# Differential attention on Trainium2: the scores of both maps on half the array each, queries and keys loaded whole, values stored by head

## The chip, the cores and the metric

The kernel runs on one core of a Trainium2 chip. The metric is device time in microseconds (us) for one execution; three runs of the kernel before are given, and one further execution was recorded by the hardware profiler. Engines are named as in the profile: PE is TensorE (matmuls), PEld its weight loads, DVE is VectorE, ACT is ScalarE, POOL is GpSimd, and SP (SyncE) is the queue from which nearly all DMA transfers are issued.

## The reference

The program is one layer of a decoder with 1024 positions and a model width of 1024. A normalized input is projected to three branches (a gated MLP over chunks, a pooling mixer and a causal differential attention), the branches are weighted by gates and projected, and a gated feed-forward layer follows. The change concerns the attention. Each of 4 heads has two maps (c = 0, 1) with 64 columns of query and key each, and one value of 128 columns:

```python
def block(args):
    qi, i = args                                   # one block of 128 queries
    ...
    s = jnp.einsum('bqhcd,bkhcd->bhcqk', qi, k).astype(jnp.float32) * scale
    s = s + bias.transpose(2, 0, 1)[None, :, None]
    s = jnp.where((rel >= 0)[None, None, None], s, -1e30)
    p = jax.nn.softmax(s, axis=-1)
    a = p[:, :, 0] - lam * p[:, :, 1]
    return jnp.einsum('bhqk,bkhd->bqhd', a.astype(v.dtype), v)
```

## The kernel before

A product of two fp32 matrices is made of fp32r matmuls: each operand is split into a high part (hi, the value rounded to fp32r) and a low part (lo, the rest), and three of the four products are added up (PASSES: hi x hi, hi x lo, lo x hi). All the large products use Strassen's scheme and run on L191.

Ahead of the attention, `store_qk` writes queries and keys of a head to DRAM (qk_d), hi and lo apart, 128 rows each: rows 0 to 63 belong to the first map, rows 64 to 127 to the second. `values` writes the value of all heads, position by position, to v_d. `rel_bias` makes the position bias with three small matmuls of 33 rows (L390); the bias tile T of a head is read back from DRAM (fsc).

The attention stage works on 32 tiles: 4 heads times 8 blocks of 128 queries, in an order given by hand (`tiles`). A tile whose block is number i has W = 128 (i + 1) key columns, in chunks of at most 512. For a tile and a map, `scores` takes a PSUM bank per chunk, and two matmuls of 128 rows: the stationary operand qs holds the map's query hi in rows 0 to 63 and lo in rows 64 to 127; the moving operand kh holds the key's hi twice, kl its lo twice. So each matmul adds two of the four products. VectorE adds the bias and finds the row's minimum in one instruction (a custom reduction, L762), and frees the bank; ScalarE does the exponential (L768).

`combine` (VectorE) subtracts the second map from the first, `transpose` turns the result on TensorE (tile at, L1103) and ScalarE copies it (ah), and `attend` multiplies it with the values (tile ms, L1112; an fp32 product, which the trace shows as two matmuls each). Between them one step of `merge_ab`, the filler, is issued per tile: six matmuls of the merge of the other two branches into a bank mm (L191), whose result VectorE multiplies into the gates ga or gb (L1179). `sub_norm` normalizes a head's output and transposes it (L1140), into a bank mm too. In each pass of the loop the steps are called in this order: scores of map 0, transpose, filler, scores of map 1, combine of the tile before, transpose. A scheduler then settles the order on each engine, as the operands become ready by its own reckoning; engines execute that order as it stands. The eight PSUM banks of the stage are 3 for scores, 2 at, 1 ms, 2 mm. The first tile's first scores are issued earlier, inside the last Strassen product of the stage before, into banks called m.

`load_head` is called one head ahead. It loads into a pool of 34 buffers of 512 KB (`a4`), each SP transfer in the order in which it stands. After the tiles `merge_c` merges the attention branch (L1204), and the product with w_out begins.

Of the kernel before, what the change touches and what calls it, by code (L numbers as in the profile page):

```python
# [11 lines left out]
F32 = mybir.dt.float32  # L12
I32 = mybir.dt.int32
F32R = mybir.dt.float32r
AF = mybir.ActivationFunctionType
# [3 lines left out]
P = 128  # L19
# [3 lines left out]
NH = 512  # L23
DFF = 2816
FT = DFF // P
NHEAD = 4
# [21 lines left out]
def trunk_kernel(  # L48
# [34 lines left out]
    def a4(shape=None, dt=F32, n="a"):  # L83
        return ap_.tile(shape or [P, S], dt, tag="a", name=nm(n))
# [7 lines left out]
    def tiny(n, tag, bufs=4):  # L92
        return sm.tile([P, n], F32, tag=tag, name=nm(tag), bufs=bufs)
# [398 lines left out]


    qk_d = dram.tile([8, 2, P, S], F32, name="qk_d")
    v_d = dram.tile([8, P, NH], F32, name="v_d")
    y_d = dram.tile([4, P, S], F32, name="y_d")
    g_d = dram.tile([24, P, S], F32, name="g_d")
    x1_d = dram.tile([KT, P, S], F32, name="x1_d")
# [3 lines left out]
    def values():  # L502

        (a11, a12), (a21, a22) = w_V
        TT, sub = nc.vector.tensor_tensor, ALU.subtract

        def operand(raw):
            hi, lo = w4(dt=F32R, n="wh"), w4(dt=F32R, n="wl")
            split(hi, lo, raw)
            return hi, lo  # L510

        def prod(banks, w, tn, first, more):
            for t in range(4):
                for j in range(4):
                    x, y = [o[:, t * P:(t + 1) * P] for o in h.T[j][tn]], wsl(w, j, 256)
                    dst = banks[t // 2][:, t % 2 * 256:t % 2 * 256 + 256]
                    if first and j == 0 and t % 2 == 0:

                        opens = nc.tensor.matmul(dst, lhsT=x[0], rhs=y[0], start=True, stop=False,
                                                 skip_group_check=True)  # L520
                    elif first and j == 0:
                        with tc.issue_after(opens.ins):
                            nc.tensor.matmul(dst, lhsT=x[0], rhs=y[0], start=False, stop=False, skip_group_check=True)
                    if first and j == 0:
                        for a, b in PASSES[1:]:
                            nc.tensor.matmul(dst, lhsT=x[a], rhs=y[b], start=False, stop=False, skip_group_check=True)
                    else:
                        mm3(dst, x, y, False, j == 3, True)

        def copies(dst, banks):  # L530
            for b in range(2):
                nc.scalar.copy(dst[b], banks[b])
            return dst

        def store(o, banks, c, r, i):

            for b in range(2):
                TT(out=o[b], in0=banks[b], in1=c[b], op=ALU.add)
                for t in range(2):
                    sl = o[b][:, t * 256:(t + 1) * 256]  # L540
                    nc.scalar.mul(sl, sl, R8[:, 4 * i + 2 * b + t:4 * i + 2 * b + t + 1])
                tt = 4 * i + 2 * b
                nc.sync.dma_start(out=v_d[tt:tt + 2, :, r * 256:(r + 1) * 256].rearrange("t p c -> p t c"),
                                  in_=o[b].rearrange("p (t c) -> p t c", t=2))

        def wide(n):
            t = w4([P, 2, NH], n=n)
            return [t[:, 0, :], t[:, 1, :]]

        A11, A12 = operand(a11), operand(a12)  # L550
        b1, b2 = ([pb1() for _ in range(2)] for _ in range(2))
        prod(b1, A11, "B11", True, True)
        c1 = copies([c2("v") for _ in range(2)], b1)
        yield
        s1, s2 = w4(n="s1"), w4(n="s2")
        TT(out=s1, in0=a21, in1=a22, op=ALU.add)
        TT(out=s2, in0=s1, in1=a11, op=sub)
        prod(b2, A12, "B21", True, False)
        store(c1, b2, c1, 0, 0)
        S1 = operand(s1)  # L560
        yield
        b3 = [pb1() for _ in range(2)]
        prod(b3, S1, "T1", True, True)
        S2 = operand(s2)
        TT(out=a21, in0=a11, in1=a21, op=sub)
        TT(out=a12, in0=a12, in1=s2, op=sub)
        yield
        prod(b1, S2, "T2", False, True)
        k2 = copies(wide("c2"), b1)
        S3 = operand(a21)  # L570
        yield
        prod(b1, S3, "T3", False, True)
        k3 = copies(wide("c3"), b1)
        store([c2("v") for _ in range(2)], b3, k3, 1, 1)
        A22 = operand(a22)
        yield
        b4 = [pb1() for _ in range(2)]
        prod(b4, A22, "T4", True, False)
        store(k3, b4, k3, 1, 0)
        S4 = operand(a12)  # L580
        yield
        prod(b3, S4, "B22", False, True)
        store(k2, b3, k2, 0, 1)
        yield
# [121 lines left out]

    def load_head(hd):

        H = heads[hd] = dict(qkl=[])
        for c in range(2):  # L710
            q, kh, kl = (a4(dt=F32R, n=n) for n in ("qs", "kh", "kl"))
            r = slice(64 * c, 64 * c + 64)
            for dst, src in ((q[0:64], qk_d[hd, 0, r]), (q[64:128], qk_d[hd, 1, r]),
                             (kh[0:64], qk_d[4 + hd, 0, r]), (kh[64:128], qk_d[4 + hd, 0, r]),
                             (kl[0:64], qk_d[4 + hd, 1, r]), (kl[64:128], qk_d[4 + hd, 1, r])):
                nc.sync.dma_start(out=dst.bitcast(F32), in_=src)
            H["qkl"].append((q, kh, kl))
            if c == 0:
                H["T"] = a4(n="T")
                base = fsc[hd]  # L720
                skew = bass.AP(tensor=base.tensor, offset=base.offset + P - 1, ap=[[NREL - 1, P], [1, S]])
                nc.sync.dma_start(out=H["T"], in_=skew)
            yield
        H["V"] = a4([P, 8, P], n="V")
        nc.sync.dma_start(out=H["V"], in_=v_d[:, :, hd * P:(hd + 1) * P].rearrange("t p c -> p t c"))
        yield
        H["s0"], H["ss"] = tiny(8, "s0", 2), tiny(8, "so", 2)
        H["O"] = a4([P, 8, P], n="O")
# [7 lines left out]
    st, AH = {}, {}  # L736
    score_bank = [pm1]

    def scores(t, c):

        if t >= len(tiles):
            return
        hd, i = tiles[t]
        H = heads[hd]
        W = (i + 1) * P
        if c == 0:
            if W <= NH:
                b = a4([P, 2, NH], n="sc")
                st[t] = dict(pr=[b[:, 0, :], b[:, 1, :]], s=[])
            else:  # L750
                st[t] = dict(pr=[a4(n="sc"), a4(n="sc")], s=[])
        q, kh, kl = H["qkl"][c]
        sc_ = st[t]["pr"][c]
        mx = tiny(2, "mx")
        chunks = [(0, min(NH, W))] + ([(NH, W - NH)] if W > NH else [])
        for n_, (c0, n) in enumerate(chunks):
            ps = score_bank[0]()
            qs = q[:, i * P:(i + 1) * P]
            nc.tensor.matmul(ps[:, :n], lhsT=qs, rhs=kh[:, c0:c0 + n], start=True, stop=False)  # L759
            nc.tensor.matmul(ps[:, :n], lhsT=qs, rhs=kl[:, c0:c0 + n], start=False, stop=True)  # L760
            o = (7 - i) * P + c0
            nc.vector.tensor_tensor_reduce(  # L762
                out=sc_[:, c0:c0 + n], in0=ps[:, :n], in1=H["T"][:, o:o + n], scale=1.0,
                scalar=mx[:, 0:1] if n_ else 3.0e38,
                op0=ALU.add, op1=ALU.min, accum_out=mx[:, n_:n_ + 1])
        nm_ = mx[:, n_:n_ + 1]
        sum_ = H["s0"][:, i:i + 1] if c == 0 else tiny(1, "s1")
        nc.scalar.activation(out=sc_[:, :W], in_=sc_[:, :W], func=AF.Exp, bias=nm_, scale=-1.0, accum_out=sum_)  # L768
        st[t]["s"].append(sum_)

    for n_ in range(12):
        Fs = strassen_pair(w_gate[n_], h, pb1)
# [299 lines left out]
    def pt2(tag, bufs):  # L1072
        def f():
            return p2.tile([P, NH], F32, tag=tag, name=nm(tag), bufs=bufs)
        return f

    score_bank[0], pat, pms, pmm = pt2("sc", 3), pt2("at", 2), pt2("ms", 1), pt2("mm", 2)

    def combine(t):

# [115 lines left out]
    def merge_c(banks):  # L1196
        for n_, (j, m) in enumerate((j, m) for j in (1, 0) for m in range(KT)):
            for k in range(3):
                pre_c(m + k)
            ps = banks[n_ % len(banks)]()  # L1200
            for ki in range(NHEAD):
                mm3(ps, wsl(wcs[m], ki), ycv[ki][j], ki == 0, ki == NHEAD - 1)
            gc = gcs[m][:, half(j)]
            nc.vector.tensor_tensor(out=gc, in0=ps, in1=gc, op=ALU.mult)  # L1204
            accumulate(mg[m][:, half(j)], gc)
            yield

    wo = strassen_full(lambda k: mg[k], w_out, 4, xT, lambda d, j: x1[d][:, half(j)], done1)
    LL = 4
    mc = merge_c([pmm, pmm, *score_bank * 3, pat, pat])  # L1210
    lates = []
    for t in range(len(tiles) + 3):
        hd, i = tiles[min(t, 31)]
# [323 lines left out]
```

## Time and profile before

| | us |
|---|---|
| median of 3 runs | 1388.32 |
| lowest, highest | 1386.16, 1389.51 |
| profiled execution, device time | 1389.13 |
| its span in the trace | 1387.4 |
| PE busy | 1344.9 (97%) |
| DVE busy | 964.5 (70%) |
| ACT busy | 652.4 (47%) |
| POOL busy | 495.9 (36%) |

The profiled execution's device time contains its span and 1.7 us around it. Busy time of PE is the union of its matmuls, the ends of which are modelled: the length shown for one matmul (0.39 us for 512 columns) is more than the distance to the next one behind it, so a stretch in which PE is busy throughout can still hold short stalls. The score matmuls of the attention run from 436.7 to 585.5 us of the span.

### The profile page before, as it was taken

The page shows a single profiled execution, that of the slowest core. Times are in us where ns is not written, and L with a number is a line of the kernel's source. Part 1 is how long each engine was busy: PE and PEld are TensorE (multiplying, and loading weights), DVE is VectorE, ACT ScalarE, POOL GpSimd, SP SyncE. Part 2 cuts the span into 40 slices and gives each one's busy share as a digit, 9 for nine tenths or more (in the row PEclk, how much of TensorE's full clock was granted, in tenths as well). Part 3 has the DMA queues.
Part 4 walks back from the last instruction along what each step waited for, and adds up shares of the span by engine and source line. Part 5 has one row for each costly group of instructions (what it writes and reads, how often), then busy time and mean ns, then how long its engine had stood idle before and what let it go on. Part 6 is the DMA issues. An engine that isn't in the chain of part 4 may idle for free.

```text
span 1387.4 us, 17666 instructions
## 1 busy us (share of the span) xinstructions
PE 1344.9 (97%) x6454; PEld 1120.5 (81%) x6454; DVE 964.5 (70%) x1487; ACT 652.4 (47%) x1109; POOL 495.9 (36%) x327
## 2 busy tenths in 40 slices
PE   9999999999999989999999999999999999999997
PEld 7997778888887778877777888888888887878786
DVE  7985774445444879958769576666777669985853
ACT  8633343344433666723667343433343435455461
POOL 0022334455553000022221665666656640102014
PEclk9999999999999999999999999999999999999998
DMA  7023363333239898588795222212222248845853
GB/s 261 10 78 109 108 222 134 121 121 104 101 115 272 252 242 209 151 233 193 201 221 131 83 77 91 79 74 91 91 77 91 75 151 305 274 126 150 226 128 122
DMA packets 78831, 204.65 MB, mean 148 GB/s; under 512 B 8270, under 2 KB 17614, under 8 KB 78744
## 3 DMA queue, kind: packets, MB, share of 16 engines
q1 hardware_dynamic: 67224, 180.44, 39.4%
q0 software_dynamic: 11520, 23.07, 9.7%
q8 instruction: 51, 0.84, 0.2%
q14 instruction: 36, 0.29, 0.1%
HBM read 143.70 MB, written 47.46 MB: 138 GB/s over the span
## 4 chain that ended last, share of the span: by engine, by line
PE 67%; DVE 13%; DMA 10%; issue 6%; ACT 3%; POOL 1%; SPq 1%; DVEq 0%; POOLq 0%; ACTq 0%
PE b L191 59%; PE mm L191 2%; DMA fr<-in_w_down 2%; DMA pr<-in_w_proj 1%; DVE ft L97 1%; PE ms L1112 1%; DVE fw L97 1%; DMA qs<-qk_d 1%; POOL ga L104 1%; DMA fr<-in_w_out 1%; DVE sc L762 1%; DMA x<-in_xT 1%; DMA yr<-y_d 1%; PE sc L759 1%; ACT fw L96 1%
## 5 line engine op out<-in xcount | busy, mean ns | idle before, releaser
L191 PE MATMUL b<-ft,fw 128*128 128x512 f32 (+1 forms) x1308 | 293.0, 384 | 9.8 <-ACT x L912 3.4
L191 PEld LDWEIGHTS b<-ft,fw 128*128 128x128 f32 x1308 | 239.9, 189 | 60.3 <-DVE fw L97 4.0
L354 POOL TENSOR_TENSOR F<-F,RB 128x1024 f32<-128x1024 f32 x68 | 185.5, 2730 | 111.3 <-DVE F L262 110.2
L262 DVE TENSOR_TENSOR F<-b,c 128x512 f32<-128x512 f32 x152 | 100.9, 683 | 130.5 <-ACT c L281 58.3
L191 PE MATMUL b<-hb,Ah 128*128 128x512 f32 x608 | 190.2, 392 | 0.0
L191 PE MATMUL b<-T,Sh 128*128 128x512 f32 x504 | 155.8, 390 | 1.9 <-ACT c L272 1.9
L234 POOL TENSOR_TENSOR s<-r 128x512 f32<-128x512 f32 x36 | 54.4, 1512 | 224.3 <-DMA r<-in_w_up 84.2
L191 PEld LDWEIGHTS b<-hb,Ah 128*128 128x128 f32 x608 | 114.5, 189 | 24.0 <-issue 0.5
L191 PE MATMUL b<-hb,Al 128*128 128x512 f32 x304 | 119.5, 393 | 2.5 <-DVE Al L97 2.5
L97 DVE TENSOR_TENSOR Al<-r,Ah 128x1024 fp32r<-128x1024 f32 x38 | 56.1, 1476 | 94.0 <-issue 77.9
L97 DVE TENSOR_TENSOR Sl<-s,Sh 128x1024 fp32r<-128x1024 f32 x76 | 107.0, 1408 | 13.9 <-ACT Sh L96 8.5
L96 ACT CAST Sh<-s 128x1024 fp32r<-128x1024 f32 x76 | 80.0, 1052 | 75.6 <-PE b L191 43.2
L191 PEld LDWEIGHTS b<-T,Sh 128*128 128x128 f32 x504 | 94.6, 188 | 21.8 <-ACT c L272 2.4
L191 PE MATMUL b<-T,Sl 128*128 128x512 f32 x252 | 98.1, 389 | 0.0
L191 PE MATMUL b<-hb,Sh 128*128 128x512 f32 x304 | 94.1, 391 | 2.9 <-DVE F L262 2.9
L96 ACT CAST Ah<-r 128x1024 fp32r<-128x1024 f32 x38 | 39.9, 1049 | 110.9 <-PE b L191 104.0
L96 ACT CAST fw<-fr 128x512 fp32r<-128x512 f32 x90 | 54.8, 622 | 62.4 <-DVE fw L97 25.0
L191 PE MATMUL b<-Th,Sh 128*128 128x512 f32 x204 | 79.1, 391 | 0.8 <-ACT c L267 0.8
L191 PE MATMUL b<-Tl,Sh 128*128 128x512 f32 x204 | 79.5, 390 | 0.0
L191 PE MATMUL b<-Th,Sl 128*128 128x512 f32 x204 | 79.4, 389 | 0.0
L191 PEld LDWEIGHTS b<-hb,Sh 128*128 128x128 f32 x304 | 56.8, 188 | 16.6 <-DVE F L262 4.2
L191 PEld LDWEIGHTS b<-hb,Al 128*128 128x128 f32 x304 | 57.4, 189 | 15.3 <-DVE Al L97 2.9
(284 smaller groups left out, 2838.9 us busy)
## 6 DMA issues: line engine op xcount, KB each, us to landing
fr<-in_w_down SPq DMA_DIRECT2D x47, 512.0 KB, 3.8
r<-in_w_up SPq DMA_DIRECT2D x42, 512.0 KB, 3.5
r<-in_w_gate SPq DMA_DIRECT2D x24, 512.0 KB, 3.6
g_d<-F SPq DMA_DIRECT2D x24, 512.0 KB, 2.8
act_d<-cv SPq DMA_DIRECT2D x22, 512.0 KB, 2.8
act<-act_d SPq DMA_DIRECT2D x22, 512.0 KB, 7.8
fr<-in_w_out SPq DMA_DIRECT2D x18, 512.0 KB, 6.1
ssb<-sq POOLq DMA_DIRECT2D x24, 256.0 KB, 4.1
```

What stands on the lines that cost most here:

```text
L96: nc.scalar.copy(hi, src)
L97: (eng or nc.vector).tensor_tensor(out=lo, in0=src, in1=hi.bitcast(F32), op=ALU.subtract)
L104: nc.gpsimd.dma_start(out=dst, in_=src, accum_op=ALU.add)
L191: last_mm[0] = nc.tensor.matmul(ps, lhsT=w[a], rhs=x[b], start=first and i == 0, stop=last and i == 2, skip_group_check=more)
L234: eng.tensor_tensor(out=s1[:, :NH], in0=a21, in1=a22, op=ALU.add)
L262: nc.vector.tensor_tensor(out=o, in0=ps, in1=c, op=ALU.add)
L354: (eng or nc.gpsimd).tensor_tensor(out=F, in0=F, in1=RB, op=ALU.mult)
L759: nc.tensor.matmul(ps[:, :n], lhsT=qs, rhs=kh[:, c0:c0 + n], start=True, stop=False)
L762: nc.vector.tensor_tensor_reduce(out=sc_[:, c0:c0 + n], in0=ps[:, :n], in1=H["T"][:, o:o + n], scale=1.0, scalar=mx[:, 0:1] if n_ else 3.0e38,
L1112: nc.tensor.matmul(po[:, :P], lhsT=AH[t][:, kb, :], rhs=H["V"][:, kb, :], start=kb == 0, stop=kb == i)
```

## The change

Queries and keys are loaded as they lie in DRAM: one tile q with hi of both maps (rows 0 to 63 and 64 to 127), one with lo, and the same for k. `scores` is called by chunk (n_) instead of by map: it takes two banks, and issues for each of the three passes one matmul per map, of 64 rows each, map 0 on rows 0 to 63 and map 1 on rows 64 to 127. The product lo x lo is no longer computed. A chunk of both maps then takes six matmuls of 64 rows where there were four of 128. The exponential follows when the last chunk of a tile is reduced. Score banks go from 3 to 4, mm from 2 to 1. The values lie in DRAM by head, so that a head's tile V is one contiguous row of 4 KB for each partition; storing them takes two transfers where there was one.

```diff
@@ -492,7 +492,7 @@
 
 
     qk_d = dram.tile([8, 2, P, S], F32, name="qk_d")
-    v_d = dram.tile([8, P, NH], F32, name="v_d")
+    v_d = dram.tile([NHEAD, P, 8, P], F32, name="v_d")
     y_d = dram.tile([4, P, S], F32, name="y_d")
     g_d = dram.tile([24, P, S], F32, name="g_d")
     x1_d = dram.tile([KT, P, S], F32, name="x1_d")
@@ -540,8 +540,9 @@
                     sl = o[b][:, t * 256:(t + 1) * 256]
                     nc.scalar.mul(sl, sl, R8[:, 4 * i + 2 * b + t:4 * i + 2 * b + t + 1])
                 tt = 4 * i + 2 * b
-                nc.sync.dma_start(out=v_d[tt:tt + 2, :, r * 256:(r + 1) * 256].rearrange("t p c -> p t c"),
-                                  in_=o[b].rearrange("p (t c) -> p t c", t=2))
+                for k in range(2):
+                    nc.sync.dma_start(out=v_d[2 * r + k, :, tt:tt + 2, :],
+                                      in_=o[b].rearrange("p (t k c) -> p k t c", t=2, k=2)[:, k])
 
         def wide(n):
             t = w4([P, 2, NH], n=n)
@@ -706,15 +707,13 @@
 
     def load_head(hd):
 
-        H = heads[hd] = dict(qkl=[])
+        H = heads[hd] = dict(q=[], k=[])
         for c in range(2):
-            q, kh, kl = (a4(dt=F32R, n=n) for n in ("qs", "kh", "kl"))
-            r = slice(64 * c, 64 * c + 64)
-            for dst, src in ((q[0:64], qk_d[hd, 0, r]), (q[64:128], qk_d[hd, 1, r]),
-                             (kh[0:64], qk_d[4 + hd, 0, r]), (kh[64:128], qk_d[4 + hd, 0, r]),
-                             (kl[0:64], qk_d[4 + hd, 1, r]), (kl[64:128], qk_d[4 + hd, 1, r])):
-                nc.sync.dma_start(out=dst.bitcast(F32), in_=src)
-            H["qkl"].append((q, kh, kl))
+            q, k = a4(dt=F32R, n="q"), a4(dt=F32R, n="k")
+            nc.sync.dma_start(out=q.bitcast(F32), in_=qk_d[hd, c])
+            nc.sync.dma_start(out=k.bitcast(F32), in_=qk_d[4 + hd, c])
+            H["q"].append(q)
+            H["k"].append(k)
             if c == 0:
                 H["T"] = a4(n="T")
                 base = fsc[hd]
@@ -722,7 +721,7 @@
                 nc.sync.dma_start(out=H["T"], in_=skew)
             yield
         H["V"] = a4([P, 8, P], n="V")
-        nc.sync.dma_start(out=H["V"], in_=v_d[:, :, hd * P:(hd + 1) * P].rearrange("t p c -> p t c"))
+        nc.sync.dma_start(out=H["V"], in_=v_d[hd])
         yield
         H["s0"], H["ss"] = tiny(8, "s0", 2), tiny(8, "so", 2)
         H["O"] = a4([P, 8, P], n="O")
@@ -736,37 +735,43 @@
     st, AH = {}, {}
     score_bank = [pm1]
 
-    def scores(t, c):
+    def scores(t, n_):
+
 
         if t >= len(tiles):
             return
         hd, i = tiles[t]
         H = heads[hd]
         W = (i + 1) * P
-        if c == 0:
+        c0 = n_ * NH
+        n = min(NH, W - c0)
+        if n <= 0:
+            return
+        if n_ == 0:
+            st[t] = dict(s=[], mx=[tiny(2, "mx", 6) for _ in range(2)])
             if W <= NH:
                 b = a4([P, 2, NH], n="sc")
-                st[t] = dict(pr=[b[:, 0, :], b[:, 1, :]], s=[])
+                st[t]["pr"] = [b[:, 0, :], b[:, 1, :]]
             else:
-                st[t] = dict(pr=[a4(n="sc"), a4(n="sc")], s=[])
-        q, kh, kl = H["qkl"][c]
-        sc_ = st[t]["pr"][c]
-        mx = tiny(2, "mx")
-        chunks = [(0, min(NH, W))] + ([(NH, W - NH)] if W > NH else [])
-        for n_, (c0, n) in enumerate(chunks):
-            ps = score_bank[0]()
-            qs = q[:, i * P:(i + 1) * P]
-            nc.tensor.matmul(ps[:, :n], lhsT=qs, rhs=kh[:, c0:c0 + n], start=True, stop=False)
-            nc.tensor.matmul(ps[:, :n], lhsT=qs, rhs=kl[:, c0:c0 + n], start=False, stop=True)
-            o = (7 - i) * P + c0
+                st[t]["pr"] = [a4(n="sc"), a4(n="sc")]
+        ps = [score_bank[0]() for _ in range(2)]
+        for k, (a, b) in enumerate(PASSES):
+            for c in range(2):
+                r = slice(64 * c, 64 * c + 64)
+                nc.tensor.matmul(ps[c][:, :n], lhsT=H["q"][a][r, i * P:(i + 1) * P], rhs=H["k"][b][r, c0:c0 + n],
+                                 start=k == 0, stop=k == 2)
+        o = (7 - i) * P + c0
+        for c in range(2):
+            sc_, mx = st[t]["pr"][c], st[t]["mx"][c]
             nc.vector.tensor_tensor_reduce(
-                out=sc_[:, c0:c0 + n], in0=ps[:, :n], in1=H["T"][:, o:o + n], scale=1.0,
+                out=sc_[:, c0:c0 + n], in0=ps[c][:, :n], in1=H["T"][:, o:o + n], scale=1.0,
                 scalar=mx[:, 0:1] if n_ else 3.0e38,
                 op0=ALU.add, op1=ALU.min, accum_out=mx[:, n_:n_ + 1])
-        nm_ = mx[:, n_:n_ + 1]
-        sum_ = H["s0"][:, i:i + 1] if c == 0 else tiny(1, "s1")
-        nc.scalar.activation(out=sc_[:, :W], in_=sc_[:, :W], func=AF.Exp, bias=nm_, scale=-1.0, accum_out=sum_)
-        st[t]["s"].append(sum_)
+            if c0 + n == W:
+                sum_ = H["s0"][:, i:i + 1] if c == 0 else tiny(1, "s1")
+                nc.scalar.activation(out=sc_[:, :W], in_=sc_[:, :W], func=AF.Exp, bias=mx[:, n_:n_ + 1], scale=-1.0,
+                                     accum_out=sum_)
+                st[t]["s"].append(sum_)
 
     for n_ in range(12):
         Fs = strassen_pair(w_gate[n_], h, pb1)
@@ -1074,7 +1079,7 @@
             return p2.tile([P, NH], F32, tag=tag, name=nm(tag), bufs=bufs)
         return f
 
-    score_bank[0], pat, pms, pmm = pt2("sc", 3), pt2("at", 2), pt2("ms", 1), pt2("mm", 2)
+    score_bank[0], pat, pms, pmm = pt2("sc", 4), pt2("at", 2), pt2("ms", 1), pt2("mm", 1)
 
     def combine(t):
 
@@ -1207,7 +1212,7 @@
 
     wo = strassen_full(lambda k: mg[k], w_out, 4, xT, lambda d, j: x1[d][:, half(j)], done1)
     LL = 4
-    mc = merge_c([pmm, pmm, *score_bank * 3, pat, pat])
+    mc = merge_c([pmm, *score_bank * 4, pat, pat])
     lates = []
     for t in range(len(tiles) + 3):
         hd, i = tiles[min(t, 31)]
```

The order of instructions after scheduling shows what the diff alone doesn't. The first place is TensorE in the stage of the second head, at a tile of 768 columns. Before, a pair of matmuls (L759 with kh, L760 with kl) serves one map and one bank; here the second map's two chunks (512 and 256 columns), between a filler's last matmul and the value products:

```order
L191 MATMUL mm_4161<-yv_3644,ph_4014 128x512
L759 MATMUL sc_4170<-kh_3845,qs_3844 128x512
L760 MATMUL sc_4170<-kl_3846,qs_3844 128x512
L759 MATMUL sc_4174<-kh_3845,qs_3844 128x256
L760 MATMUL sc_4174<-kl_3846,qs_3844 128x256
L1112 MATMUL ms_4154<-V_3550,ah_4098 128x128 x3
```

After the change, the same tile's second chunk and the first of the next tile. The moving tile k_3776 is the key's hi and k_3854 its lo, q_3775 and q_3853 the query's; the bank tells the map: sc_4191 and sc_4243 are the first map's (rows 0 to 63), sc_4192 and sc_4244 the second's (rows 64 to 127):

```order
L191 MATMUL mm_4127<-yv_3632,ph_4033 128x512
L761 MATMUL sc_4191<-k_3776,q_3775 128x256
L761 MATMUL sc_4191<-k_3854,q_3775 128x256
L761 MATMUL sc_4191<-k_3776,q_3853 128x256
L1117 MATMUL ms_4122<-V_3548,ah_4064 128x128 x4
L761 MATMUL sc_4192<-k_3776,q_3775 128x256
L761 MATMUL sc_4192<-k_3854,q_3775 128x256
L761 MATMUL sc_4192<-k_3776,q_3853 128x256
L761 MATMUL sc_4243<-k_3776,q_3775 128x512
L761 MATMUL sc_4243<-k_3854,q_3775 128x512
L761 MATMUL sc_4243<-k_3776,q_3853 128x512
L761 MATMUL sc_4244<-k_3776,q_3775 128x512
```

The three passes of a map stand together, and full-array matmuls stand between the two maps of the first chunk, though the code issues the maps in turn. At a few places, as at the first tiles, the maps do alternate.

The second place is TensorE at the sub-norm of a head (transposes of O into a bank mm). Before, the transposes follow a pair of scores, and the filler behind them has a bank of its own:

```order
L759 MATMUL sc_4334<-kh_3845,qs_3844 128x256
L760 MATMUL sc_4334<-kl_3846,qs_3844 128x256
L1140 MATMUL mm_4288<-ident,O_3554 128x128 x4
L191 MATMUL mm_4324<-yv_3638,ph_4014 128x512
L191 MATMUL mm_4324<-yv_3639,ph_4014 128x512
```

After the change, with one bank mm, the transposes stand right behind a filler's matmuls:

```order
L191 MATMUL mm_4351<-yv_3638,ph_4033 128x512
L191 MATMUL mm_4351<-yv_3644,ph_4033 128x512
L191 MATMUL mm_4351<-yv_3645,ph_4033 128x512
L191 MATMUL mm_4351<-yv_3644,ph_4033 128x512
L1145 MATMUL mm_4374<-ident,O_3552 128x128 x4
L761 MATMUL sc_4480<-k_3776,q_3775 128x384
```

The transposes into mm_4374 can begin only when VectorE has read mm_4351.

## Rows read from the trace of the kernel before

**Rows 1.** Busy us (instructions) by stretch; then PE clock, DMA share, GB/s.

```profile
444.00:462.00 18.00, 15.67 (x57) 11.21 (x58) 15.50 (x32) 9.48 (x14) 4.79 (x2) 0.91 0.72 279
...
480.00:500.00 20.00, 14.55 (x72) 11.60 (x71) 14.24 (x43) 10.81 (x35) 0.86 (x1) 0.91 1.05 288
500.00:590.00 90.00, 89.24 (x580) 78.52 (x578) 82.69 (x278) 64.55 (x197) 4.30 (x5) 1.00 0.75 187
```

**Rows 2.** Timeline of PE from 527 us: start, length, instruction, count.

```profile
527.12 1.06 PE L1112 MATMUL ms<-V,ah 128*128 128x128 f32 x8
527.93 0.42 PE L759 MATMUL sc<-kh,qs 128*128 128x384 f32 x1
528.19 0.34 PE L760 MATMUL sc<-kl,qs 128*128 128x384 f32 x1
528.37 1.09 PE L191 MATMUL mm<-yv,ph 128*128 128x512 f32 x4
...
529.75 0.28 PE L759 MATMUL sc<-kh,qs 128*128 128x256 f32 x1
529.87 0.27 PE L760 MATMUL sc<-kl,qs 128*128 128x256 f32 x1
```

**Rows 3.** Groups of PE instructions from 500 to 590 us: busy, mean ns, idle before.

```profile
L191 PE MATMUL mm<-yv,ph 128*128 128x512 f32 x126 | 33.5, 400 | 0.0
L1112 PE MATMUL ms<-V,ah 128*128 128x128 f32 x204 | 28.5, 277 | 0.2 <-ACT sq L1117 0.2
L1103 PE MATMUL at<-ident,sc 128*128 128x128 f32 x108 | 16.5, 274 | 0.0
L759 PE MATMUL sc<-kh,qs 128*128 128x512 f32 x27 | 11.7, 434 | 0.3 <-DVE mx L762 0.2
...
L759 PE MATMUL sc<-kh,qs 128*128 128x384 f32 x10 | 3.7, 365 | 0.0
...
L759 PE MATMUL sc<-kh,qs 128*128 128x128 f32 x12 | 3.3, 272 | 0.0
```

**Rows 4.** Timeline of PE from 480 to 500 us, in brackets idle time before.

```profile
484.75 0.47 PE L760 MATMUL sc<-kl,qs 128*128 128x512 f32 x1 [1.59 <-DMA kl<-qk_d]
...
493.37 2.07 PE L191 MATMUL mm<-yv,ph 128*128 128x512 f32 x4 [3.32 <-ACT ph L96]
```

**Rows 5.** Chain that ended last, two pieces: start, us, what.

```profile
106.93 23.78 PE b L191 x110
...
480.30 12.38 DMA pr<-in_w_proj
```

**Rows 6.** Bias matmuls L390: timeline of PEld and PE; last, min, median, max ns.

```profile
130.10 0.19 PEld L191 LDWEIGHTS b<-hb,Al 128*128 128x128 f32 x1
...
130.32 0.39 PE L191 MATMUL b<-hb,Al 128*128 128x512 f32 x1
130.64 1.02 PE L390 MATMUL m<-oh,rb 33*4 33x512 f32 x2
131.59 0.73 PE L191 MATMUL b<-hb,Sh 128*128 128x512 f32 x2
...
140.15 0.39 PE L191 MATMUL b<-Th,A 128*128 128x512 f32 x1
140.47 0.38 PE L390 MATMUL m<-oh,rb 33*4 33x127 f32 x2
...
L390 PE MATMUL m<-oh,rb x6: 268/589/589, 130.6 to 140.6; 33*4 33x512 f32 x4, 33*4 33x127 f32 x2
```

**Rows 7.** Group of the filler's multiply on DVE, 436 to 592 us.

```profile
L1179 DVE TENSOR_TENSOR ga<-mm,ga 128x512 f32<-128x512 f32 x16 | 11.0, 686 | 3.2 <-PE mm L191 2.2 <-DMA ga<-g_d 1.0
```

**Rows 8.** DMA from 421 to 515 us: packets and bytes; issues of one kind.

```profile
DMA packets 9985, 24.56 MB, mean 261 GB/s; under 512 B 1056, under 2 KB 4128, under 8 KB 9980
...
kh<-qk_d SPq DMA_DIRECT2D x12, 256.0 KB, 10.1
```

**Rows 9.** Issues of value stores on SP: min, median, max ns; first, last start.

```profile
L543 SPq DMA_DIRECT2D v_d<-v x4: 360/374/390, 71.8 to 93.2; - x4
```

## The prediction

> **What bounds the kernel now.** I read the stretches first [rows 1]: between 500 and 590 us, where most score tiles are worked on, the reader is to see TensorE busy for 89.24 of 90 us, VectorE for 82.69, and the DMA engines with room (0.75). Busy can hide stalls, because the ends of matmuls are modelled, so I rebuilt those 90 us from spacings. Four matmuls of 512 columns take 1.09 us, a single one 0.39, so they follow each other by 0.23; one of 384 columns is followed after 0.18, one of 256 after 0.12; eight of 128 columns take 1.06 with a last one of 0.28, which is 0.11 each [rows 2]. Times the counts [rows 3], where the second matmul of each score pair (L760) has the counts of the first and 256 columns the count of 384: 126 x 0.23 for mm, (204 + 108) x 0.11 for ms and at, another 24 x 0.11 for the transposes of L1140, and 54, 20, 20 and 24 score matmuls at 0.23, 0.18, 0.12 and 0.11. That is 29.0 + 37.0 + 21.1 = 87 us of 90. TensorE is full there: what is added to it lengthens the kernel. VectorE has 7 us to spare.
>
> From 480 to 500 us it is otherwise: TensorE is busy for 14.55 of 20 us, and DMA is saturated at 1.05 [rows 1]. A score pair waits 1.59 us for kl, a merge matmul 3.32 us for weights [rows 4], whose load is on the chain that ended last for 12.38 us [rows 5]. From 444 to 462 us VectorE is nearly full (15.50 of 18), TensorE is not (15.67). In both stretches the mean granted clock is 0.91 [rows 1]: the lower level, 1.2 of 2.4 GHz, for part of the time.
>
> Ahead of attention and from the first w_out products on, the change leaves the order on TensorE, VectorE, ScalarE and GpSimd as it is; only SyncE's value stores differ there.
>
> **The score matmuls themselves.** Before there are 192: 12 chunks a head, two maps, two matmuls each, which is 96, 32, 32 and 32 of 512, 384, 256 and 128 columns. At the spacings above they take 22.1 + 5.8 + 3.8 + 3.5 = 35.2 us. Afterwards there are 288, each on 64 rows. The spacing goes with the columns in these rows, so without overlap they take half as much again: +17.6.
>
> How much overlaps is decided by the order: for most tiles the scheduler does not leave the two maps alternating. It issues the three passes of one map, which share 64 rows and one bank and so must follow each other, then the three of the other. Only where a matmul on the other half comes next can two run at once. In the 45 unbroken runs of score matmuls I counted 77 such neighbours: 37 of 512 columns, 19 of 384, 9 of 256, 12 of 128. No row here shows matmuls on different halves, so what one neighbour saves lies between nothing and its whole streaming time. For 512 columns that is 37 x 0.23 = 8.5 us. Each matmul needs its weight load, and the runs of 128 columns show that loads come no faster than one in 0.11 us, so a pair costs at least 0.22: 384 columns save 19 x (0.36 - 0.22) = 2.7, shorter ones nothing. I take the full 11 us, because the halves share neither rows nor banks. Streaming then adds +6.6 us; the ends are +6.6 and +17.6.
>
> **The switch between 128-row and 64-row matmuls.** The 45 runs are entered from and left to full-array matmuls: 90 switches. The trace has one small relative, the bias matmul of 33 rows by 4 columns between full-array ones [rows 6]. The matmul ahead of it starts at 130.32; the next would start at 130.55, and it starts at 130.64 together with its weight load. Loads of full-array matmuls run ahead (that of Al at 130.10, its matmul at 130.32). So 0.09 us is lost, and a 128-column load would stand open as well. Leaving: two passes spaced by 0.43 (1.02 less 0.589) end at 131.50, the next matmul starts at 131.59, and the first pair takes 0.73 where spacing and length make 0.62 (0.23 + 0.39): 0.09 + 0.11 lost. Another entry shows the same 0.32 (140.15 to 140.47). With 128-column loads each way costs 0.20, a run 0.40, 45 runs 18 us; with the small load as measured 0.29 a run, 13 us. Between fp32 and fp32r matmuls nothing is lost: from 527.12 to 528.19 lie eight spacings of 0.11 and one of 0.18 [rows 2]. So it goes with the shape, not with the type. I take 18, since score loads have 128 columns; the ends are 0 (columns alone matter) and 18.
>
> The Trainium skill (TensorEngine Tiling (Array Packing), Key Properties) says that changing the tiling mode, not just the tile, drains the engine. The entries in this trace agree, for the one shape that it has. By that rule the sum keeps its 18 us; if only the bias matmul's 4 columns were the cause, it would be 18 lower.
>
> **Banks.** Score banks go from 3 to 4, mm from 2 to 1. In the new order two mm groups stand 2 us of TensorE work or more apart, except that at five places the sub-norm's transposes follow directly on a filler. With one bank they wait for the end of the filler's last matmul (0.39 - 0.23) and its multiply (0.69 [rows 7]), and all of TensorE behind them, the next scores above all: 5 x 0.85 = 4.3 us. The ends are 0 (TensorE had to wait for VectorE anyway) and twice that, where the multiply stands behind another VectorE piece of that length. I take 4.3.
>
> **Loads.** A head's queries and keys go from twelve loads of 256 KB to four of 512 KB, 3 to 2 MB. Between 421 and 515 us there are loads for three heads (kh x12 and as many qs and kl) among 24.56 MB at 261 GB/s [rows 8]. 3.1 MB less is 12 us of DMA time, more than the two waits. V becomes one contiguous row a partition, part of the same relief. It can give back the idle time of 480 to 500 us, 20 - 14.55 = 5.4, and the slow clock, (1 - 0.91) x 20 = 1.8 [rows 1]. I take 7; the lower end is 0. After 500 TensorE does not wait for loads.
>
> The value stores become 16 of half the size, eight more issues of some 0.37 us each on SyncE [rows 9]. TensorE's unbroken run of 110 matmuls from 106.93 to 130.71 [rows 5] covers the last of them: 0, and 3 us if all eight stood open.
>
> From 444 to 462 us TensorE's 2.3 idle us and (1 - 0.91) x 18 = 1.6 of slow clock [rows 1] take up extra TensorE work, since VectorE's reductions set the pace and stay as they are. I take 3 of the 3.9; the ends are 0 and 3.9.
>
> **Sum**: +6.6 + 18 + 4.3 - 7 - 3 = +18.9 us. The profiled execution took 1389.1 us, 0.8 over the median of 1388.32; so 1408.
>
> **Rivals.**
> *Cheap switches, not slower* (0.24). If going from 128 to 64 rows with all 128 columns costs nothing, the sum is 18.9 - 18 = +0.9: 1390.0, no change; from 0.02 us a run it turns slower by what can be told (1391.1). Without the bank waits it is -3.4, 1385.7. For it: no row shows this very shape. Against: equal losses at both entries, a load that never ran ahead.
> *The halves do not overlap* (0.16): the change then doesn't do what its words say, +29.9, 1419. For it: every matmul in the trace follows the last at streaming time. Against: all of those share rows.
> *Weights of a half load only while it is idle* (0.08): each of the 288 - 77 - 45 = 166 matmuls behind one of its own half then shows its 0.11 us load, +18, 1426. Against it: the full-array loads run ahead [rows 6]. The Trainium skill (TensorE: Matmul & The Clock Gate, Part 3, The mechanism) says that weight loads overlap running matmuls only where the row group differs; the full-array loads here contradict it.
>
> **Chances.** The likeliest, 0.52, lies from 1398 to 1418: 0.29 us a run, no bank waits and the whole relief, or nothing relieved or hidden. Of the cheap-switch case I put 0.11 below 1385.5, 0.09 within 0.2% of the median (about what a measurement of this kernel tells from no change), 0.04 above. So slower is 0.52 + 0.16 + 0.08 + 0.04 = 0.80. The range from 1387 to 1421 leaves out the third rival and the faster part of the first, about 0.2.
>
> **What the profile would show.** Switches: at every border of a run a weight load that starts about 0.1 us after the matmul before it has streamed, not ahead of its matmul. Overlap: at a change of map the next start follows within some hundredths, while the three passes of one map lie 0.23 apart. Banks: transposes after a filler that wait for the multiply into ga or gb. Relief: no wait for keys or merge weights between 480 and 500. From 500 on VectorE's busy share falls while its work stays. I am wrong if runs of scores begin without a gap, or if the stage up to the first merge into the score banks (L1204) is no longer than now.

## The result and the profile after

Six executions of the changed kernel took 1394.31 to 1403.85 us, median 1398.24; six of the kernel before 1383.66 to 1389.51, median 1386.58. The ratio is 1.0089, 95% interval 1.0063 to 1.0114: slower by 11.7 us in the medians, where I forecast 1408 and a range of 1387 to 1421. The profiled execution took 1397.2 us, its span 1395.5, which is 8.1 more than the profiled one of before; that one lay 2.6 above the median of its six, this one 1.0 below. What is read from the two traces below is therefore an account of 8.1 us, not of 11.7.

The whole difference arises between the first score into the stage's own banks (446.8 us before, 445.9 after) and the last matmul of the attention's merge (639.6 and 648.6): 192.8 us have become 202.7. Behind it, compared matmul by matmul, the distance of the two traces moves between 4.9 and 9.2 us, and is 8.1 at the end. The stretches of [rows 1], after the change (columns as there):

```profile
444.00:462.00 18.00, 15.34 (x82) 10.90 (x81) 15.22 (x33) 7.59 (x13) 5.12 (x2) 0.91 0.36 126
480.00:500.00 20.00, 20.00 (x128) 15.35 (x128) 17.50 (x55) 13.50 (x39) 0.86 (x1) 1.00 0.73 226
500.00:590.00 90.00, 85.32 (x552) 67.01 (x550) 70.07 (x228) 53.15 (x166) 3.45 (x4) 1.00 0.48 138
```

From 480 to 500 us TensorE is now busy throughout, at the full clock, and DMA has room (0.73 for 1.05). From 500 on VectorE is busy for 70 of 90 us where it was 83: the stage goes slower through the same work. From 444 to 462 us nothing became better: 15.34 us busy for 15.67, and the clock still 0.91.

The timeline of TensorE's matmuls at one run of twelve score matmuls shows both the switch and the overlap:

```profile
522.26 0.49 PE L1108 MATMUL at<-ident,sc 128*128 128x128 f32 x3
522.59 0.39 PE L1117 MATMUL ms<-V,ah 128*128 128x128 f32 x2
522.90 1.50 PE L761 MATMUL sc<-k,q 64*128 64x512 f32 x12
524.34 0.50 PE L191 MATMUL mm<-yv,ph 128*128 128x512 f32 x1
```

and the weight loads of the same stretch:

```profile
522.48 0.30 PEld L1117 LDWEIGHTS ms<-V,ah 128*128 128x128 f32 x2
522.90 1.17 PEld L761 LDWEIGHTS sc<-k,q 64*128 64x128 f32 x12
524.33 0.30 PEld L191 LDWEIGHTS mm<-yv,ph 128*128 128x128 f32 x2 [0.26 <-issue]
```

At both borders load and matmul start together (522.90, 524.33), where loads of full-array matmuls run ahead [rows 6]. The twelve (six of 512 columns, six of 384) and the way back take 524.34 - 522.90 = 1.44 us. One behind the other they would need 6 x 0.23 + 6 x 0.17 = 2.4 without any switch. So six streams of two must run, although the order has three of one map ahead of three of the other. Where only one map's three stand in a run, they take as long as six of both elsewhere (both of 512 columns):

```profile
516.46 0.96 PE L761 MATMUL sc<-k,q 64*128 64x512 f32 x3
...
518.93 0.97 PE L761 MATMUL sc<-k,q 64*128 64x512 f32 x6
```

The transposes that stand behind a filler wait for the only mm bank, here and in the waits of TensorE from 440 to 660 us (total, times, longest):

```profile
512.97 0.66 PE L1145 MATMUL mm<-ident,O 128*128 128x128 f32 x4 [0.79 <-DVE gb L1184]
```

```profile
PE mm L1145 <- DVE gb L1184: 2.4, 3, 0.8
...
PE mm L1145 <- DVE ga L1184: 1.6, 2, 0.8
```

For an account of the stage I took the distance of every matmul to the next start in the two traces and subtracted the spacing of its columns (0.23, 0.17, 0.12, 0.11 us); a pair that starts together counts once. At the borders of the 43 runs of the stage (two more belong to the first tile, ahead of it) the median lateness is 0.09 us going in and 0.10 coming back, with an open weight load of 0.11 and 0.10: 0.40 a run.

| us, of the stage | before | after | change | forecast |
|---|---|---|---|---|
| score matmuls at their spacing | 33.8 | 33.4 | -0.4 | +6.6 |
| 43 runs by 0.40 | 0 | 17.2 | +17.2 | +18 |
| five transposes behind a filler | 0 | 4.75 | +4.75 | +4.3 |
| waits and slow clock, 470 to 500 us | 8.6 | 0 | -9.0 | -7 |
| the same, 440 to 460 us | 5.5 | 5.3 | -0.2 | -3 |
| all other waits | 5.7 | 3.5 | -2.2 | 0 |
| sum | | | +10.2 | +18.9 |

(The -9.0 includes -0.4 by which the spacings overshoot there.) The sum is within 0.3 us of the 9.9 that the landmarks give.

### The profile page after: what moved, and what is told of

Read it like the earlier page. It is cut to its first block, busy times and chain, and to the rows that moved or that the text cites. A ratio compares the mean times of both kernels' runs of the same rounds, so it can differ in the third digit from the quotient of the medians.

```text
span 1395.5 us, 17809 instructions
## 1 busy us (share of the span) xinstructions
PE 1355.6 (97%) x6550; PEld 1117.3 (80%) x6550; DVE 970.3 (70%) x1487; ACT 650.9 (47%) x1109; POOL 495.0 (35%) x327
```

## The experiments

My theory after the result: two halves (64 of the array's 128 rows each) stream together whatever their order in a run, the switches cost 17 us, the bank wait 5, and the relief of 470 to 500 us is one of bytes. The rivals: switches are cheap and the loss lies elsewhere; only neighbours overlap; the relief has another source. Each kernel ran with the kernel before on the same chip, whose medians were 1384.3 to 1386.3 us; what is compared is the ratio to it, with its 95% interval.

**All rows for each score matmul** (changed kernel):

```diff
-                r = slice(64 * c, 64 * c + 64)
+                r = slice(0, P)
```

> The changed kernel with every score matmul on all 128 rows (the same 288 matmuls in the same 45 runs, banks, loads and order; a score then adds up both maps, so the scores are not those of the reference). My theory: the switches (43 runs in the trace by 0.40, 17 us, and 3 to 5 us of waits at them) go, and the overlap is lost (33.4 us of streaming become the 52.8 us of 288 matmuls, +19.4): 1397 to 1402 us, and the trace shows no late weight loads and no pairs. Rival one, switches cheap and the loss elsewhere: only the overlap is lost, 1417. Rival two, the overlap is worth little and the switches cost all: 1376 to 1381.

Measured: 1400.91 us, 1.0109 (1.0086 to 1.0132), so as the theory said; the changed kernel's 1.0089 cannot be told from it. The run shown above becomes, in its timeline:

```profile
523.28 0.39 PE L1117 MATMUL ms<-V,ah 128*128 128x128 f32 x2
523.42 2.71 PE L761 MATMUL sc<-k,q 128*128 128x512 f32 x12
525.97 0.86 PE L191 MATMUL mm<-yv,ph 128*128 128x512 f32 x3
```

2.55 us from start to start instead of 1.44, with nothing lost at its borders. Score matmuls of the stage take 50.8 us at their spacing instead of 33.4, and the switches are gone: what overlap gives (17.4) and what switching takes (17.2) cancel. The time alone would not separate the two; the trace does.

**Two banks as one tile, and the sub-norm's transposes.** The first edit gives both maps' banks out together, so that the scheduler alternates the maps in every run and no run has one map alone; the second moves the transposes of L1145 into an at bank.

```diff
-        ps = [score_bank[0]() for _ in range(2)]
+        ps = score_bank[0]()
...
+    def psc():
+        b = p2.tile([P, 2, NH], F32, tag="sc", name=nm("sc"), bufs=2)
+        return [b[:, 0, :], b[:, 1, :]]
```

```diff
-            lates.append(sub_norm(tiles[u][0], (0, 1), pmm))
+            lates.append(sub_norm(tiles[u][0], (0, 1), pat))
```

> The changed kernel with the two score banks of a chunk as one tile of two banks (two buffers), so that both maps become ready together: in the order the maps then alternate in all runs, 36 runs instead of 45, none with one map alone. My theory: 9 runs fewer save 9 x 0.40 = 3.6 us, and with the 84 lone score matmuls paired streaming falls from 33.4 to 26.1 us: 1398.2 - 10.9 = 1387 us. Rival: a bank pair is free only when VectorE has reduced both, and TensorE waits there for what it saves: 1395 to 1400. Second rival, neighbours alone overlap (as forecast), so alternating maps save far more than 7 us against maps in blocks: but then the changed kernel could not show blocks of three and three in pairs; under 1383.

> The changed kernel with the sub-norm's transposes in an at bank in place of the only mm bank. The order moves with it: 47 runs instead of 45. My theory: the five waits behind a filler, 4.75 us, go, two more runs cost 0.8: 1394 us. Rival: VectorE is what TensorE waits for, and the wait turns up at the next at or score bank: 1398.

> Both together, the bank pair and the sub-norm's transposes in an at bank; 40 runs in the order. My theory: against the bank pair alone 4.75 us less for the waits and 4 x 0.40 more for the runs: 1384 us, below the kernel before. Rival: the same as the bank pair alone or slower, 1387 to 1391, if the waits only move.

Measured: the bank pair 1395.67 us, 1.0075 (1.0047 to 1.0103); the transposes in at 1392.32, 1.0046 (1.0030 to 1.0063); both 1384.69, 0.9990 (0.9973 to 1.0007). The second and third expectations held within 2 us; the first did not, and its time lies where the rival had put it. The bank pair's score matmuls did fall to 25.4 us at their spacing, in 34 runs of the stage, but at the sub-norm a second wait grew beside the old one. Its timeline of TensorE at two such places:

```profile
501.62 0.66 PE L1158 MATMUL mm<-ident,O 128*128 128x128 f32 x4
503.53 0.66 PE L1121 MATMUL at<-ident,sc 128*128 128x128 f32 x4 [1.26 <-ACT ah L1122]
...
508.86 0.66 PE L1158 MATMUL mm<-ident,O 128*128 128x128 f32 x4 [0.78 <-DVE gb L1197]
```

The at transposes behind the sub-norm's wait for ScalarE to copy ah, six times, 6.2 us in all; in the changed kernel that was four times and 1.9 us. With both edits the trace has neither wait, and the gain of alternating shows. My rival had put the new wait at the bank pair itself; it is at the sub-norm.

**Order within a run** (the kernel with both edits; before, the loop over passes was the outer one):

```diff
+        mms = []
+        for c in range(2):
+            r = slice(64 * c, 64 * c + 64)
+            for k, (a, b) in enumerate(PASSES):
+                mm = nc.tensor.matmul(...)
+                if mms:
+                    tc.add_manual_dep(mm.ins, mms[-1].ins.name, ...)
+                mms.append(mm)
```

> The fourth experiment's kernel (bank pairs, sub-norm in an at bank) with one thing changed: within each run the three passes of the first map are issued ahead of the three of the second (AAABBB), by added ordering, instead of in turn (ABABAB); 40 runs either way, same banks. The forecast's step, only a neighbour on the other half overlaps: of six matmuls of 512 columns five slots remain instead of three, 48 chunks by two slots of 0.11 to 0.23, +16.9 us: 1401 to 1402 us. Rival, from the trace of the changed kernel: a half's matmuls start ahead of the other half's that were issued before them, and the order in a run is worth nothing: the same as the alternating kernel, 1384 to 1386.

> The alternating kernel (ABABAB) again, beside its block order on the same chip: 1384 to 1386 us.

Measured: in blocks 1386.13 us, 1.0010 (0.9995 to 1.0025); alternating 1386.84, 1.0020 (1.0005 to 1.0035). The same run in the timeline of either, in blocks first:

```profile
519.86 1.51 PE L762 MATMUL sc<-k,q 64*128 64x512 f32 x12
521.29 0.55 PE L1126 MATMUL at<-ident,sc 128*128 128x128 f32 x3
```

```profile
520.74 1.50 PE L761 MATMUL sc<-k,q 64*128 64x512 f32 x12
522.17 0.55 PE L1121 MATMUL at<-ident,sc 128*128 128x128 f32 x3
```

1.43 us in both. By the forecast's step five slots of each size would stand there, less one where the two blocks meet: 5 x 0.23 + 5 x 0.17 - 0.17 = 1.8, and 0.2 for the borders. The order within a run is worth nothing. The alternating kernel is the one that was measured above: its ratio was 0.9990 on one chip and is 1.0020 on another, 0.30% apart, so that the two intervals barely meet, and 1386.84 lies above what I expected. A difference of that size between kernels that ran on different chips is therefore not shown by the ratios alone.

**Where the relief comes from.** One kernel puts the bytes back into the changed kernel; one takes the values alone into the kernel before; one takes the lo of the keys away as well, so that the kernel before has the bytes of the changed one.

```diff
+            q, k, x = a4(dt=F32R, n="q"), a4(dt=F32R, n="k"), a4(dt=F32R, n="x")
+            for dst, src in ((q, qk_d[hd, c]), (k, qk_d[4 + hd, c]), (x, qk_d[4 + hd, c])):
+                for r in (slice(0, 64), slice(64, 128)):
+                    nc.sync.dma_start(out=dst[r].bitcast(F32), in_=src[r])
```

> The changed kernel with the bytes of before: each head loads its keys a second time into a further tile that nobody reads, and queries and keys go in halves of 256 KB, so twelve transfers and 3 MB a head again. The scheduler makes 49 runs of it instead of 45 (+1.6 us). My theory, the relief of 480 to 500 us comes from the bytes: the waits for keys and merge weights are back there, 5 to 7 us, so 1404 to 1407 us. Rival: it comes from the values by head, the fourth score bank, or from TensorE being later than the loads anyway: 1398 to 1400.

> The kernel before with the values in DRAM by head, and nothing else. My theory, bytes of queries and keys make most of the relief: 1384 to 1386 us. Rival, the values' pieces of 512 bytes held up the loads behind them: the waits of 480 to 500 us (5 us) go, 1381.

```diff
-            q, kh, kl = (a4(dt=F32R, n=n) for n in ("qs", "kh", "kl"))
+            q, kh = (a4(dt=F32R, n=n) for n in ("qs", "kh"))
+            kl = kh
```

> The kernel before with the values by head and without the tile kl: both matmuls of a score pair read kh, so that a head has 2 MB of queries and keys as in the changed kernel, but the 192 full-array score matmuls, the banks and the switch-free TensorE of before (the key's lo is left out of the scores, so they are not those of the reference). Theory, bytes alone give the relief: the 7 to 8 us that TensorE waits between 470 and 500 us go, 1378 to 1380 us. Rival, in the changed kernel TensorE is later there, by the switches, and meets the loads for that reason: half of the waits or more stay, 1382 to 1386.

Measured: bytes back 1403.80 us, 1.0131 (1.0111 to 1.0151); values alone 1386.29, 1.0007 (0.9993 to 1.0022); without kl 1382.14, 0.9971 (0.9956 to 0.9986). The stretches 480:490 and 490:500 of the three, in this order (columns as in [rows 1]):

```profile
480.00:490.00 10.00, 10.00 (x53) 6.88 (x51) 7.71 (x22) 4.01 (x13) 0.00 (x0) 1.00 1.03 286
490.00:500.00 10.00, 10.00 (x63) 7.40 (x62) 9.27 (x26) 8.34 (x25) 0.86 (x1) 1.00 1.04 267
```

```profile
480.00:490.00 10.00, 7.43 (x42) 5.70 (x40) 7.16 (x23) 4.21 (x15) 0.86 (x1) 1.00 1.04 306
490.00:500.00 10.00, 7.93 (x37) 6.73 (x38) 7.34 (x20) 6.46 (x17) 0.00 (x0) 0.83 1.04 266
```

```profile
480.00:490.00 10.00, 9.54 (x59) 7.43 (x58) 9.50 (x35) 8.94 (x29) 0.86 (x1) 1.00 1.04 293
490.00:500.00 10.00, 9.99 (x64) 8.63 (x63) 10.00 (x35) 7.80 (x22) 0.00 (x0) 1.00 1.04 273
```

With the bytes back DMA is full again (1.03), the time came near what I expected (1404 to 1407), but not by the way that I expected: TensorE does not wait. The merge weights, whose load ended at 492.68 before [rows 5], are split by ScalarE from 487.58 us on in the changed kernel and from 491.98 with the bytes back. So the bytes do set when they arrive; the order, made with those loads, has other TensorE work in front of them. By the ratios this kernel is 5.8 us slower than the changed one (1.0131 against 1.0089, four executions). Its trace shows 1.6 for four more runs and 1.3 for fewer pairs, which is what its profiled execution (1399.86) lies above that of the changed kernel (1397.2); but that execution is 3.9 us below its median, and the rest is in no trace.

The values alone are worth nothing that can be told: the waits of 470 to 500 us are 7.7 us, by the account above, for 8.6. Without kl they are 3.6 us, and the kernel is 0.36% faster than with the values alone, some 5 us (on another chip). So fewer bytes, with full-array scores as before, take about half of these waits: the measured 1382.1 lies at the edge of the rival's span. None of the waits that are left is for a load; the longest is 1.0 us for VectorE's multiply into gb. The rest is gone only in the changed kernel and in the one with the bytes back. How much of that is lateness by switches and how much a different order, the runs do not tell apart.

**Other ways to the relief.** The kernel before with values by head, four score banks, one mm bank and the transposes in at (the edits are shown above); and with k holding a map's hi and lo, so that a head needs 2.5 MB:

```diff
+            nc.gpsimd.memset(ql[64:128].bitcast(F32), 0.0)
+            for dst, src in ((q[0:64], qk_d[hd, 0, r]), (q[64:128], qk_d[hd, 0, r]), (ql[0:64], qk_d[hd, 1, r]),
+                             (k[0:64], qk_d[4 + hd, 0, r]), (k[64:128], qk_d[4 + hd, 1, r])):
```

> The kernel before with the values by head, four score banks and one mm bank, and the sub-norm's transposes in an at bank: the score matmuls and the loads of queries and keys stay as before. My theory: part of the waits between score matmuls of before (9.5 us between two scores in its trace) are for score banks, and a fourth takes 2 to 5 us of them: 1380 to 1384. Rival: they are all for loads and for VectorE, which is as busy as before: 1385 to 1387.

> The kernel before with the values by head, and with full-array scores of fewer bytes: the moving tile k holds a map's key hi in rows 0 to 63 and lo in rows 64 to 127 for both of its matmuls, the first stationary tile holds the query's hi twice, the second its lo and zeros (written by GpSimd): 192 score matmuls as before, no switch, 2.5 MB a head instead of 3, and no lo x lo. My theory: it keeps TensorE's 35 us of scores, pays nothing for switches, and gains half of the relief or more: 1380 to 1384 us, faster than before. Rival: the relief needs the full megabyte, or the waits are elsewhere: 1385 to 1388.

> Full-array scores with 2.5 MB a head (the eighth experiment) and the banks of the seventh (four for scores, one mm, the sub-norm in an at bank). Theory: the two gains add up, -2.7 us of the banks and -1.0 of the fewer bytes: 1381 to 1382.5, faster than both. Rival: both take from the same waits, and one of the two alone is what there is: 1383 to 1385.

Measured: banks 1382.86 us, 0.9983 (0.9972 to 0.9994); fewer bytes 1384.58, 0.9994 (0.9980 to 1.0008); both 1382.64, 0.9987 (0.9973 to 1.0001). The banks are worth 0.24% against the values alone, as expected. Fewer bytes gave less than expected, and both together came out no faster than the banks alone, though the intervals are too wide to exclude that the two add up. In the kernel with fewer bytes the stage takes 186.2 us instead of the 191.9 with the values alone, but begins 4.8 us later: TensorE waits ahead of it for VectorE's last eviction of the product before, 3.9 us instead of 1.4. From 470 to 500 us its waits are still 6.7 us by the account, for 7.7: the wait for merge weights is gone, one for keys is left, and one for VectorE's multiply into ga stands there instead. Two of its waits from 444 to 650 us, and the row of the timeline:

```profile
PE b L191 <- DVE F L262: 3.9, 1, 3.9
PE mm L191 <- DVE ga L1180: 2.3, 1, 2.3
```

```profile
487.43 0.47 PE L760 MATMUL sc<-k,qs 128*128 128x512 f32 x1 [1.44 <-DMA k<-qk_d]
```

With the banks alone, and with all 3 MB a head, the waits of 470 to 500 us fall as far as without kl, from 7.7 to 3.3 us; two of them were 1.8 and 2.7 us with the values alone:

```profile
PE sc L761 <- DMA kl<-qk_d: 1.3, 1, 1.3
PE mm L191 <- ACT ph L96: 0.7, 1, 0.7
```

So fewer bytes are one way to shorten these waits, and other banks are another. Of the kernels that compute all of the scores, that with the banks alone is the only one whose interval lies wholly under the kernel before, by 0.06 to 0.28%; the two measurements of the alternating kernel lie further apart than that.

## Why the prediction was right in direction and 10 us too high

The measured 1398.24 us stands at the lower edge of the span that I called likeliest, 1398 to 1418. That it falls inside is partly luck: the edge stood for 0.29 us a run and no bank waits, and neither came. The time lies there because streaming cost 7 us less than forecast.

**Switches**: right. 0.40 us a run was forecast from the bias matmul [rows 6] and 0.40 was measured; the first experiment shows that it is the change in the number of rows that costs, since nothing is lost at the borders when the same matmuls use all 128. Cheap switches fall with it.

**Streaming**: the term that was mis-sized. The step "Only where a matmul on the other half comes next can two run at once" failed: of six matmuls in the order AAABBB I counted one neighbour and so five slots; the trace has three. +6.6 was forecast, -0.4 measured, 7 of the 10.8 us by which the sum missed the profiled 1397.2. Some 4 of the 7 are that step: 104 pairs start together (within 0.06 us) where I had counted 77 neighbours. The other 3 are a second step, "a pair costs at least 0.22", which left the 77 at 11 us where their whole streaming time is 14. Six matmuls of 128 columns show that it failed too:

```profile
467.13 0.56 PE L761 MATMUL sc<-k,q 64*128 64x128 f32 x6
467.62 0.88 PE L1108 MATMUL at<-ident,sc 128*128 128x128 f32 x6
```

They and the way back take 0.49 us; six weight loads at one in 0.11 would alone take 0.66, so the loads of the two halves run at once as well. What limits the overlap is that 17 of the 43 runs hold one map alone. Halves that do not overlap (the second rival), and loads of a half only while it is idle (the third), are wrong: the twelve loads above take 1.17 us beside the streams.

**Banks**: right, 4.75 us for 4.3, at the five places that the order showed, each with 0.79 us idle. Taking them away gave 0.43% by the ratios, some 6 us; the intervals do not tell that from the 4 us expected.

**Relief**: about right in size, 9.0 for 7, but its cause, fewer bytes, was at most half the story: with the bytes put back into the changed kernel no wait between 470 and 500 us returned, and in the kernel before other banks shortened the waits as much as fewer bytes did. V by head, counted as part of it, is no part that can be measured.

**Early TensorE work, hidden**: the -3 did not come. The waits of 440 to 460 us stayed (5.3 for 5.5 us), since they stand at single places behind VectorE, the longest at the first scores, before and after:

```profile
449.36 0.50 PE L759 MATMUL sc<-kh,qs 128*128 128x512 f32 x1 [1.54 <-DVE mx L762]
```

```profile
448.70 1.67 PE L761 MATMUL sc<-k,q 64*128 64x512 f32 x11 [2.35 <-DVE F L262]
```

Before, TensorE waited there for VectorE's reductions of the first scores; after, for its last eviction of the product before (F). Work that is added between later matmuls does not fill such waits.

The remaining 2.2 us of other waits, and 1.8 ahead of and behind the stage, I had not foreseen.

## What to carry to other kernels

Count what two halves save against what a run on them costs: with both maps in every run a chunk of 512 columns takes three spacings of 0.23 us instead of the four that the stacked full-array form took, and one spacing saved does not earn the 0.40 us of going in and out, so by these numbers halves pay only in runs of two such chunks or more, or against a form that takes six full-array matmuls a chunk, as in the first experiment. Within a run the order needs no care, but both halves need work in it. A wait for a load can go because fewer bytes come, because the engine comes later or because other work stands in front of it, and only runs with the bytes put back, or taken from the kernel before, tell which.

## What the runs showed of the hardware

A half's matmuls start ahead of matmuls of the other half that stand before them in the order: in blocks of three the pairs of the 1.43 us run start 0.010 to 0.017 us apart; alternating, 0.004 to 0.010. Over all runs, where the first two matmuls of a run start together they are 0.010 us apart in blocks and 0.003 to 0.004 alternating; in the run shown from the changed kernel, at 522.90, they are 0.010 apart, as in blocks. So what I wrote of the kernel before, that engines execute the order as it stands, does not hold between the two halves. The Trainium skill (TensorE: Matmul & The Clock Gate, Part 3, The mechanism) says that matmuls start and end in program order without any reordering; for matmuls on different halves this case's traces show otherwise. Two streams at once cost a single one nothing: three of one half take 0.96 us, six of both 0.97.
